# Six tiles in place of four for raw weights, in the room of a halved descriptor scratch

## The chip, the cores and the metric

The kernel runs on one core of a Trainium2 chip. The metric is the device time of one execution in microseconds (us). Before the change it is 770.23 us, the median of three runs (769.88 to 770.24).

The core has a tensor engine (PE, whose weight loads are shown apart as PEld), a vector engine (DVE), a scalar engine (ACT), a general engine (POOL, GpSimd) and a queue engine (SP, SyncE) that only issues transfers here. POOL issues transfers too: those that add to what they write.

## The reference

A decoder layer over 512 tokens of width 1024, in float32, batch 1. Two token mixers run side by side from one projection and are merged by sigmoid gates; a squared-ReLU MLP and a last norm follow.

```python
h = rms_norm(x, norm_mix)
proj = h @ w_in                       # 1024 -> 512 + 1024 + 6*128 + 48 + 2048
u, q, kc, vc, ksl, vsl, kwn, vwn, g_nsa, g_merge = split(proj)
y_pool = pool_mixer(u, w_pool, pool_scale)      # causal means over 2, 4, 8, 16 tokens
y_nsa = nsa_mixer(q, kc, vc, ksl, vsl, kwn, vwn, g_nsa, pe_k, pe_v, w_ck1, w_ck2, w_cv1, w_cv2)
g_a, g_b = split(sigmoid(g_merge))
x = x + (g_a * (y_pool @ w_proj_pool) + g_b * (y_nsa @ w_proj_nsa)) @ w_out
h = rms_norm(x, norm_mlp)
x = x + square(relu(h @ w_ff1)) @ w_ff2         # 1024 -> 4096 -> 1024
out = rms_norm(x, norm_final)
```

The second mixer has 16 heads of 64 in 2 groups. Each query attends to compressed keys (an MLP over blocks of 32 tokens), to selected blocks and to a window; at 512 tokens the selection and the window take in every causal key.

## The kernel before, in words

**Precision.** Every float32 product is split: each operand becomes a high part that PE multiplies quickly and a low part, the rest. ACT writes the high part (a copy that rounds) and DVE the low part (raw minus high). A product is three matmuls: high by high, high by low, low by high. So every weight tile that arrives from HBM as raw float32 costs one ACT and one DVE operation, or two of half the size, before PE can use it.

**Weight pipeline.** LD is the list of all loads in the order in which they are wanted, most of them 128 partitions by 1024 floats (512 KB). WL is the list of weight tiles in the order in which PE uses them. `emit_load` (L278) issues the next load on SP's queue (L297) into a tile tagged `raw`; there are RAW of these (L103), and they go round. `emit_prep_half` (L494) writes the high and low halves of the next weight tile (L524 on ACT, L527 on DVE); when a tile is done, its raw tile is free and one more load is issued. `gate_steps` (L411), `wo_steps` (L461) and `group_steps` (L372) do the same for the weights of the fast matrix products below (L428/L431, L471/L474, L390/L395). `ahead` (L542) is called between groups of matmuls and prepares the next weight if a pair of target tiles (wh/wl, wkt) is free for it. The load into a raw tile that has just been split waits on SP for the end of that split. Everything behind it on SP waits as well.

**The last stage.** From load MLP0 on, tiles are handed on by name: the first RAW of these loads take over the raw tiles (L287), a further tile `raw5` comes in when the attention's memory is free (L1599), and from then on a load is issued whenever a tile is given back (L323).

**Sums of weights.** The gates' projection, the output projection and the MLP use a seven-product scheme for products of two by two blocks, which needs sums of weight blocks (S1 to S4). Some of them are made in DRAM: SP copies one block into a DRAM tile (L335) and POOL adds the other with an accumulating transfer (L343); later the sum is loaded like any other weight. When each copy and each addition is issued hangs on the number of the load being issued (`sums_after`, L311, and the conditions at L301 to L306). POOL waits at an addition until the copy has landed.

**Order.** The program is written in one order. Between groups of matmuls it steps generators (`side`) that hold the evacuations, rope, the pooling mixer and so on. A planner then fixes the order of each engine: it takes instructions by their place in the program, moves some forward where `high_priority` says so, and starts one when by its own cost model its data and its tile are ready.

**Stages, by the profile's time.** A prologue (to about 16 us) normalises and transposes x; four loads are begun in it (L759 to L767), between the loads of x and of the constants. Until about 145 us the first projection runs: compressed keys (ck, wk0 to wk3), pooled channels (u0 to u3), keys, values (V0 to V2), first queries, the MLPs that compress keys and values (L997), wpool, and the gates' seven products (psV, L638). Until about 370 us the attention runs (L1378, L1400, L1410, L1423, L1440, L1474) with the rest of the projection as filler. Then the output projections, and from about 450 us the MLP in four parts, each with a first layer (L638) and a second (L1698).

**DMA scratch.** The program object (L2076) reserves part of each SBUF partition for the descriptors of transfers that POOL issues: 16,384 bytes where nothing is said.

## Time and profile before

| | |
|---|---|
| median of three runs | 770.23 us |
| span of the profiled execution | 767.4 us |
| PE busy | 756.7 us (99%) |
| DVE busy | 666.4 us (87%) |
| ACT busy | 511.1 us (67%) |
| POOL busy | 184.2 us (24%) |
| moved on SP's queue | 122.90 MB |
| moved by POOL's transfers | 26.22 MB |

The profile is of one execution of its own, from the first to the last instruction; for that execution it gives the span and no other time, so what lies around the span is seen only against the runs: 770.23 - 767.4 = 2.83 us. A line of the profile names the source line, the engine, the operation, what is written and read, shapes and count. "Idle before" is the time in which the engine stood still just before such an instruction, with what ended it. SPq and POOLq are the issuing of transfers. A busy PE is not PE at its peak, as matmuls overlap.

### The profile page before, as it was taken

The page shows a single profiled execution, that of the slowest core. Times are in us where ns is not written, and L with a number is a line of the kernel's source. Part 1 is how long each engine was busy: PE and PEld are TensorE (multiplying, and loading weights), DVE is VectorE, ACT ScalarE, POOL GpSimd, SP SyncE. Part 2 cuts the span into 40 slices and gives each one's busy share as a digit, 9 for nine tenths or more (in the row PEclk, how much of TensorE's full clock was granted, in tenths as well). Part 3 has the DMA queues.
Part 4 walks back from the last instruction along what each step waited for, and adds up shares of the span by engine and source line. Part 5 has one row for each costly group of instructions (what it writes and reads, how often), then busy time and mean ns, then how long its engine had stood idle before and what let it go on. Part 6 is the DMA issues. An engine that isn't in the chain of part 4 may idle for free.

```text
span 767.4 us, 13409 instructions
## 1 busy us (share of the span) xinstructions
PE 756.7 (99%) x4757; PEld 675.9 (88%) x4757; DVE 666.4 (87%) x1279; ACT 511.1 (67%) x977; POOL 184.2 (24%) x264
## 2 busy tenths in 40 slices
PE   9999999999999999999999999999999999999996
PEld 7889889888888888888889899989998999889985
DVE  7897999548988889989689689997989788978897
ACT  7766655328878888898745576954774477447754
POOL 4001010117746766574000200111111110111001
PEclk9999999999999999999999999999999999999999
DMA  9559993983051833371357965989998999799942
GB/s 308 165 143 266 251 230 108 257 214 115 15 176 52 158 56 70 56 138 60 116 186 220 324 111 185 287 219 299 310 259 222 314 303 257 215 325 294 293 171 110
DMA packets 119886, 150.76 MB, mean 196 GB/s; under 512 B 5782, under 2 KB 92346, under 8 KB 119611
## 3 DMA queue, kind: packets, MB, share of 16 engines
q1 hardware_dynamic: 98250, 122.90, 48.3%
q0 software_dynamic: 21280, 26.22, 22.8%
q8 instruction: 38, 0.62, 0.3%
q10 hardware_dynamic: 288, 0.79, 0.3%
q14 instruction: 30, 0.24, 0.1%
HBM read 145.16 MB, written 54.53 MB: 260 GB/s over the span
## 4 chain that ended last, share of the span: by engine, by line
PE 84%; DVE 9%; ACT 2%; DMA 2%; issue 1%; POOL 1%; SPq 0%; DVEq 0%; ACTq 0%; POOLq 0%
PE psB L638 20%; PE psB L1698 18%; PE psF L568 16%; PE psB L568 6%; PE psV L638 5%; PE psS L1378 4%; PE psT L1440 4%; PE psO L1474 4%; PE psB L1647 3%; DMA raw<-w_in 2%; PE psF L700 1%; DVE wl L527 1%; DVE PT L1456 1%; DVE P L1400 1%; DVE wkt L527 1%
## 5 line engine op out<-in xcount | busy, mean ns | idle before, releaser
L343 POOL DMA_DIRECT2D S<-w_ff x44 | 49.0, 1113 | 351.3 <-DMA S<-w_ff 290.3
L568 PE MATMUL psF<-R,wh 128*128 128x512 f32 x384 | 124.6, 400 | 0.0
L390 ACT ACTIVATE wh<-raw 128x1024 fp32r<-128x1024 f32 x73 | 77.1, 1058 | 70.0 <-PE psB L638 24.0
L1423 POOL TENSOR_SCALAR P<-P,sm,GT 128x128 f32<-128x128 f32 (+3 forms) x128 | 85.5, 724 | 68.8 <-DVE sm L1420 36.1
L395 DVE TENSOR_TENSOR wl<-raw,wh 128x1024 fp32r<-128x1024 f32 x73 | 88.9, 1219 | 12.7 <-ACT wh L390 12.2
L568 PEld LDWEIGHTS psF<-R,wh 128*128 128x128 f32 x384 | 68.8, 188 | 11.4 <-issue 0.2
L1410 ACT ACTIVATE P<-P,sm 128x128 f32<-128x128 f32 (+3 forms) x128 | 71.0, 557 | 9.9 <-DVE sm L1400 6.2
L568 PE MATMUL psF<-R,wl 128*128 128x512 f32 x192 | 75.5, 393 | 0.0
L524 ACT ACTIVATE wh<-raw 128x512 fp32r<-128x512 f32 (+1 forms) x76 | 45.1, 616 | 32.9 <-PE psF L568 21.2
L1400 DVE CUSTOM_DVE_ANT_0 P<-psS,cst 128x128 f32<-128x128 f32 (+3 forms) x128 | 59.3, 482 | 4.9 <-PE psT L1440 2.7
L390 ACT ACTIVATE w3h<-raw 128x1024 fp32r<-128x1024 f32 x37 | 39.2, 1059 | 34.0 <-PE psB L638 12.6
L527 DVE TENSOR_TENSOR wl<-raw,wh 128x512 fp32r<-128x512 f32 (+1 forms) x74 | 51.5, 707 | 9.2 <-ACT wh L524 8.9
L1451 ACT ACTIVATE PT<-psT 128x512 fp32r<-128x512 f32 (+2 forms) x96 | 49.0, 520 | 13.9 <-PE psT L1440 13.0
L1456 DVE TENSOR_TENSOR PT<-psT,PT 128x512 fp32r<-128x512 f32 (+2 forms) x96 | 56.2, 591 | 1.5 <-ACT PT L1451 1.3
L1440 PE MATMUL psT<-ident,P 128*128 128x128 f32 x320 | 50.1, 273 | 0.6 <-POOL rx L899 0.4
L395 DVE TENSOR_TENSOR w3l<-raw,w3h 128x1024 fp32r<-128x1024 f32 x37 | 45.1, 1220 | 4.7 <-ACT w3h L390 4.5
L1474 PE MATMUL psO<-PT,VV 128*128 128x256 f32 x320 | 48.5, 286 | 0.0
L1440 PEld LDWEIGHTS psT<-ident,P 128*128 128x128 f32 x320 | 39.6, 140 | 9.4 <-POOL rx L899 0.8
L638 PE MATMUL psB<-R,wh 128*128 128x256 f32 x336 | 46.3, 279 | 0.0
L1474 PEld LDWEIGHTS psO<-PT,VV 128*128 128x128 f32 x320 | 42.2, 188 | 1.3 <-ACT PT L1451 0.3
L638 PEld LDWEIGHTS psB<-R,wh 128*128 128x128 f32 x336 | 42.5, 188 | 0.2
L568 PEld LDWEIGHTS psF<-R,wl 128*128 128x128 f32 x192 | 36.0, 188 | 7.5
(442 smaller groups left out, 2083.7 us busy)
## 6 DMA issues: line engine op xcount, KB each, us to landing
raw<-w_ff SPq DMA_DIRECT2D x54, 512.0 KB, 6.2
S<-w_ff POOLq DMA_DIRECT2D x44, 512.0 KB, 8.2
raw<-S SPq DMA_DIRECT2D x44, 512.0 KB, 5.3
S<-w_ff SPq DMA_DIRECT2D x32, 512.0 KB, 7.3
raw<-w_in SPq DMA_DIRECT2D x31, 512.0 KB, 4.7
S<-S SPq DMA_DIRECT2D x12, 512.0 KB, 6.7
raw<-w_proj_nsa SPq DMA_DIRECT2D x8, 512.0 KB, 4.1
x<-x SPq DMA_DIRECT2D x7, 512.0 KB, 6.5
```

The costliest lines, as they stand in the source:

```text
L390: ACT.activation(h, t, AF.Copy)
L395: DVE.tensor_tensor(l, t, h.bitcast(F32), op=ALU.subtract)
L527: eng.tensor_tensor(l[:, sl], t[:, sl], h[:, sl].bitcast(F32), op=ALU.subtract)
L568: PE.matmul(ps, a, b, start=first and j == 0, stop=last and j == n - 1, skip_group_check=True)
L638: PE.matmul(out, w[u][:, k, 128 * f:128 * f + 128], moving[v][:, k, :], **kw)
L1400: DVE.tensor_tensor_reduce(out=P[:, o:o + n].rearrange("p (a c) -> p a c", c=128), in0=s, in1=m, scale=1.0, scalar=3e38, op0=ALU.add, op1= ...
L1410: last_exp[:] = [ACT.activation(c, c, AF.Exp, bias=sm[:, 0, e:e + 1], scale=-1.0, accum_out=sm[:, 1, e:e + 1])]
L1423: r = POOL.tensor_scalar(P[:, o:o + n], P[:, o:o + n], sm[:, 2, e:e + 1], GT[:, qb, c + e:c + e + 1], op0=ALU.mult, op1=ALU.mult)
L1440: PE.transpose(pt[:, 128 * j:128 * j + 128], P[:, 128 * j:128 * j + 128], ident)
L1456: return DVE.tensor_tensor(dL, src, dH.bitcast(F32), op=ALU.subtract)
L1474: PE.matmul(ps[:, qb % 2, :, :], VV[:, k, b, g, :], t[:, j, :, :], start=False, stop=last and j == len(kbs) - 1 and t is tL, skip_group_ch ...
L1698: PE.matmul(ps[f], self.Y.of(y)[u][:, 2 * g + k, 128 * f:128 * f + 128], w[v][:, k, :], start=first and g == k == u == v == 0, stop=g == k ...
```

## The change

RAW goes from four to six, so that six raw tiles go round, and seven with `raw5` in the last stage. Two more loads are issued at the end of the prologue, after the first halves of the first two projections and after the side work so far. The room, two tiles of 4,096 bytes in each partition, comes from the scratch for the descriptors of POOL's transfers, which is set to 8,192 bytes. All other places that use RAW follow it: the last stage takes over six tiles, and the tests `st["load"] > RAW + MLP0` and `st["kept"] == RAW` move with it. As additions and copies of the sums hang on load numbers, they are issued two loads earlier in the program too.

```diff
-    RAW = 4
+    RAW = 6
...
     next(first)
     next(first)
+    for _ in range(2):
+        emit_load()
     drain_side()
...
-    nc = bacc.Bacc("TRN2", target_bir_lowering=False, num_devices=1)
+    nc = bacc.Bacc("TRN2", target_bir_lowering=False, num_devices=1, dynamic_dma_scratch_size=8192)
```

## The prediction

> **What bounds the kernel now.** I read the page's busy times first, then busy time by stretch, then what TensorE (PE) waited for, then the instructions around its longest wait inside the work.

> ```profile
> span 767.4 us, 13409 instructions
> ...
> PE 756.7 (99%) x4757; PEld 675.9 (88%) x4757; DVE 666.4 (87%) x1279; ACT 511.1 (67%) x977; POOL 184.2 (24%) x264
> ...
> q0 software_dynamic: 21280, 26.22, 22.8%
> ...
> L524 ACT ACTIVATE wh<-raw 128x512 fp32r<-128x512 f32 (+1 forms) x76 | 45.1, 616 | 32.9 <-PE psF L568 21.2
> ...
> S<-w_ff POOLq DMA_DIRECT2D x44, 512.0 KB, 8.2
> ...
> rs<-rx SPq DMA_DIRECT2D x40, 64.0 KB, 2.0
> ```

> In the stretches the columns are the bounds and length of the stretch, then busy time and instructions of PE, PEld, DVE, ACT and POOL, the granted clock, the DMA share and GB/s.

> ```profile
> 0.00:16.00 16.00, 14.13 (x78) 10.46 (x79) 12.06 (x24) 11.60 (x22) 8.83 (x21) 1.00 0.95 311
> 16.00:32.00 16.00, 16.00 (x107) 14.44 (x106) 14.01 (x22) 13.42 (x24) 2.51 (x7) 1.00 0.66 183
> ...
> 32.00:64.00 32.00, 32.00 (x179) 28.44 (x178) 31.90 (x66) 20.18 (x37) 1.34 (x1) 1.00 0.65 186
> ...
> 80.00:96.00 16.00, 15.30 (x113) 14.34 (x112) 15.31 (x26) 10.23 (x16) 0.85 (x1) 1.00 0.93 245
> ...
> 176.00:368.00 192.00, 190.35 (x1231) 167.76 (x1230) 172.23 (x571) 164.38 (x446) 121.23 (x185) 1.00 0.38 87
> 368.00:752.00 384.00, 384.00 (x2441) 348.24 (x2441) 339.87 (x429) 236.27 (x336) 35.19 (x32) 1.00 0.86 244
> 752.00:767.40 15.40, 8.92 (x40) 7.03 (x38) 10.77 (x22) 6.86 (x20) 2.56 (x2) 0.88 0.36 137
> ```

> PE is the bound. It idles 767.4 - 756.7 = 10.7 us: 1.87 us before 16 us, 6.48 us after 752 us, and in between 0.70 us (80 to 96) and 1.65 us (the attention, 176 to 368). From 368 to 752, the output projection and the MLP, it is busy without a gap, although the DMA share there is 0.86. Deeper prefetch can only win idle time of PE that comes from late weights. So I ask what PE waited for between 16 and 752 us (total, times, longest):

> ```profile
> PE psS L1378 <- DVE sm L1400: 0.8, 2, 0.5
> PE psC L997 <- DVE wkt L527: 0.7, 1, 0.7
> PE psT L1440 <- POOL rx L899: 0.4, 1, 0.4
> PE psO L1465 <- DVE oT L1483: 0.2, 1, 0.2
> PE psT L1440 <- DVE PT L1456: 0.2, 1, 0.2
> ```

> No row names a transfer. Four are softmax, rope and evacuation work of the attention. One, 0.70 us at L997, is a weight tile whose low half (wkt) VectorE (DVE) delivered late. The instructions around it, taken from the views of four engines (start, length; in brackets the idle time before it and what ended it):

> ```profile
> 59.07 0.37 SPq L297 DMA_DIRECT2D raw<-w_in  x1
> ...
> 64.31 0.38 SPq L297 DMA_DIRECT2D raw<-w_cv  x1
> 68.33 0.37 SPq L297 DMA_DIRECT2D raw<-w_pool  x1
> ...
> 72.90 0.38 SPq L297 DMA_DIRECT2D raw<-w_in  x1
> ...
> 75.24 0.73 ACT L524 ACTIVATE wpl<-raw 128x256 fp32r<-128x256 f32 x2 [3.19 <-DMA raw<-w_pool]
> ...
> 78.29 1.06 ACT L428 ACTIVATE wh<-raw 128x1024 fp32r<-128x1024 f32 x1 [0.43 <-DMA raw<-w_in]
> ...
> 82.56 1.07 ACT L428 ACTIVATE wh<-raw 128x1024 fp32r<-128x1024 f32 x1 [1.68 <-PE psF L568]
> ...
> 75.69 0.76 DVE L527 TENSOR_TENSOR wpl<-raw,wpl 128x256 fp32r<-128x256 f32 x2 [2.02 <-ACT wpl L524]
> ...
> 85.60 1.23 DVE L431 TENSOR_TENSOR wl<-raw,wh 128x1024 fp32r<-128x1024 f32 x1
> 86.75 0.68 DVE L527 TENSOR_TENSOR wkt<-raw,wkt 128x512 fp32r<-128x512 f32 x1
> ...
> 87.95 0.68 DVE L527 TENSOR_TENSOR wkt<-raw,wkt 128x512 fp32r<-128x512 f32 x1
> ...
> 87.03 0.96 PE L997 MATMUL psC<-wkt,cA 128*128 128x256 f32 x6
> 88.69 0.50 PE L997 MATMUL psC<-wkt,cA 128*128 128x256 f32 x2 [0.70 <-DVE wkt L527]
> ```

> So there is one place where a late load reaches PE, by two steps: ScalarE (ACT) stood 3.19 us for wpool, DVE therefore stood 2.02 us, and from 75.69 on DVE works through a backlog until 88.63 with some 0.5 us of pause. PE loses 0.70 us at its end.

> **The change part by part.**

> *Six tiles and two more loads.* Nothing is computed more or less: the same loads of 512 KB, splits and matmuls. A finished split begins one load in the freed tile, so the waits of SP stay where they are and the load behind each becomes the one two places later in the list: load i is issued when load i-2 was. Wpool is number 19 and moves from 68.33 to the place of number 17, 59.07; number 20, the w_in load of 72.90, moves to that of number 18, 64.31. Wpool's load had landed when ACT began at 75.24, at most 6.9 us after its issue; at 59.07 it lands by 66.0, and ACT's 3.19 us and DVE's 2.02 us go. The w_in load's 0.43 us of ACT goes as well. Then the chain behind: ACT's conversion at 82.56 waits for PE and stays, so its DVE half (85.60) can start at 83.63 at the earliest, 1.97 us sooner, and the two wkt halves behind it follow by nearly as much, if DVE's order stays. PE wants the last at 87.99 and it would end at 88.63 - 1.97 = 86.7. The wait falls to nothing: **-0.70 us**. What is late next at that place is PE itself.

> Bounds of this term: 0, if DVE's backlog is refilled by other work, and -0.70, as no more is waited there. I take -0.70, because 1.97 is well over 0.70.

> *Sums.* The copies into DRAM and POOL's accumulating transfers for the sums S1 to S4 hang on load numbers, so they move two loads earlier as well, in the same order on SP and POOL. The tightest case is the gates' S2:

> ```profile
> 77.31 1.03 POOL L343 DMA_DIRECT2D S_g<-S_g  x1 [9.76 <-DMA S_g<-w_in]
> ...
> SPq L297 <- DMA S_g<-S_g: 2.3, 1, 2.3
> ```

> Its load held SP for 2.3 us until the sum had landed, and four rope copies stood behind it. Its copy begins some 9 us sooner now, while its load moves up by two places, about 6 to 8 us; that wait shrinks. PE did not feel it: 0 us. Cover gone, it would be 2.3 us on rope's copies, with PE still in the gates' matmuls.

> *Prologue.* Loads 4 and 5 need no freed tile any more, and two more follow them: about 1 MB more is in flight by 16 us. At the 311 GB/s of the first stretch that is 3.4 us of transfer. The next stretch shows DMA idle for 0.34 of 16 us, 5.4 us, so it fits in there. All of it is issued behind x, the first four weights and the constants on SP's queue, so the start of PE doesn't move: 0. Behind the loads on SP come rope's copies of the first k:

> ```profile
> 27.02 2.51 SPq L882 DMA_DIRECT2D rs<-rx  x4
> ...
> 34.81 0.41 DVE L899 TENSOR_TENSOR rs<-rs,cst 128x256 f32<-128x256 f32 x1
> ```

> They are issued by 29.53 and used at 34.81, which leaves 5.3 us less the landing (2.0 us is its median); even the full 3.4 us would nearly be absorbed. Bounds 0 to +0.1; I take 0.

> *Attention, output projection, MLP.* Here no wait of PE names a weight. Seven tiles in place of five (with the extra one of the last stage) let loads run further ahead, 0 us. Cover gone, a late tile of the MLP would cost PE what ACT waits, and PE shows none. For the shift of the attention's small waits in either direction, bounds -1.65 us (all its idle time) and, for a loss of like size, +1.65 us; I take 0, since their releasers are DVE and POOL results.

> *Smaller scratch.* It moves the constants by 8,192 bytes and the raw tiles grow by two of 4,096, so nothing shifts by an odd amount: 0. [...]

> Sum: 767.4 - 0.70 = 766.7 us of span. The median of the runs is 770.23, 2.83 us over the profiled span, which I take as what lies around it: 766.7 + 2.83 = **769.5 us**.

> **The rivals.**

> *A. No change, 770.2.* The loads begin earlier, but DVE's freed 2 us are filled by other work that the planner then finds ready, or another wait takes the place. For it: between 32 and 64 us DVE is busy 31.90 of 32 us and so has work queued. Against: at 73 us it idled with nothing to do.

> *B. All of PE's inner idle time shrinks, 767.9.* 770.23 - (0.70 + 1.65) = 767.88. For it: attention work is ordered by the same planner, and small waits move when anything before them does. Against: weights arrive long before their use there.

> *C. Slower: splits go ahead of what PE needs, 772.3.* The planner places instructions by when it believes their data is there. Weights that are there two loads sooner let splits of two more tiles, four halves of 0.68 us on DVE (the row of 86.75), come ahead of a result that PE waits for. DVE has only 0.1 us of room between 32 and 64 us, so that 4 x 0.68 = 2.7 us come back as a wait of PE: 770.23 + 2.7 - 0.70 = 772.3. It decides as soon as the halves moved ahead exceed PE's lead over DVE, which was below zero at 88 us. Against: a split also needs a free target, and ACT's 21.2 us of waiting for PE at L524 shows that targets come late, not data.

> [...]

> **How the numbers follow.** The forecast has 0.44, A 0.20, B 0.17, C 0.16, D 0.03. What this kernel's measurement can tell from no change is about 0.2%, 1.54 us. The forecast (-0.7) and A lie within it, B is faster, C and D slower; of the forecast's chance I leave 0.02 to each side. Same: 0.44 + 0.20 - 0.04 = 0.60; faster 0.17 + 0.02 = 0.19; slower 0.16 + 0.03 + 0.02 = 0.21. The likeliest case alone spans 768.8 to 770.2 (twice the gain, or none). The range runs from B less the 0.4 us by which the runs shown differ, 767.5, to C, 772.3; D and half of C's and a part of B's spread lie outside, under 0.2.

> **What would show it.** In the changed trace: wpool's load issued near 59 and the next w_in near 64 us; no wait of ACT for wpool; DVE without the 2.02 us of idle; no wait of PE at L997; PE full from 16 to 176 us and from 368 to 752 us as before; PE's busy time before 16 us still near 14.1; adds of POOL no slower than 1.2 us. I am wrong if PE shows a new wait behind a split of DVE before 176 us (C), if the sum of attention waits moves by over 1 us (B or its reverse), or if POOL's adds come spaced by their landing (D).

## The result, and the profile after

The changed kernel takes 778.35 us (median, 777.68 to 779.32) beside 770.24 us for the kernel before on the same chip: a ratio of 1.0105, 95% interval 1.0089 to 1.0121. It is **8.1 us slower**. The forecast was 769.5 us, and its range ended at 772.3. One of the ten executions of run e3 below took 1257.79 us at a mean granted clock of 0.557 and is left out of that run's ratio.

The profiled execution has a span of 776.9 us and a time of its own of 778.66 us. What lies around the span is therefore 1.76 us; the prediction had taken 2.83 from the runs' median, so the execution profiled before the change was about 1.1 us quicker than its median. Below, spans are compared with spans, and by them the change costs 9.5 us and not 8.1.

The page of the changed kernel, its busy times and POOL's additions:

```profile
span 776.9 us, 13408 instructions
...
PE 761.7 (98%) x4757; PEld 679.2 (87%) x4757; DVE 667.1 (86%) x1279; ACT 510.0 (66%) x977; POOL 183.9 (24%) x264
...
L343 POOL DMA_DIRECT2D S<-w_ff x44 | 49.0, 1115 | 370.9 <-DMA S<-w_ff 294.3
```

PE has the same 4757 instructions. Of the 9.5 us, 4.5 are idle time of PE (776.9 - 761.7 = 15.2 us in place of 10.7) and 5.0 are a longer busy time (761.7 in place of 756.7). The stretches of the changed kernel say where (bounds, length, busy time and instructions of PE, PEld, DVE, ACT and POOL, granted clock, DMA share, GB/s; a transfer's packets are counted in the stretch in which they begin, so a share can pass 1):

```profile
16.00:176.00 160.00, 159.96 (x977) 143.12 (x977) 132.32 (x241) 92.61 (x161) 16.85 (x26) 1.00 0.85 222
176.00:368.00 192.00, 189.79 (x1226) 166.79 (x1225) 172.54 (x568) 163.36 (x442) 120.74 (x185) 1.00 0.38 84
368.00:464.00 96.00, 91.67 (x496) 78.79 (x495) 69.96 (x106) 48.91 (x87) 6.75 (x6) 0.96 0.67 182
464.00:752.00 288.00, 288.00 (x1909) 264.72 (x1909) 260.63 (x312) 183.07 (x245) 28.53 (x26) 1.00 0.92 260
```

Between 16 and 176 us the predicted gain is there: PE idles 0.04 us, where it had idled 0.70. The attention idles 2.21 us (1.65 before). Between 368 and 464 us, the output projection, where PE had no gap at all, it now idles 4.33 us and the clock was 0.96. The MLP is full as before.

From here on I measure stages in each trace by their first and last matmuls, to about 0.1 us: first projection, from the first product (L700) to the first scores; attention, to the start of the last product with V; output projection, from the end of that product to the last transpose before the MLP.

```
                                     first projection  attention  output projection  span
before                                          164.3      192.4               88.7  767.4
after                                           163.0      193.6               97.4  776.9
```

What the first projection won, the attention gave back: the two together take 356.6 us, and 356.7 before. The loss is in the output projection.

**First projection.** The timeline of the changed kernel shows the load and the splits that wkt had stood behind:

```profile
58.69 0.37 SPq L297 DMA_DIRECT2D raw<-w_pool  x1
...
64.50 0.37 SPq L297 DMA_DIRECT2D raw<-w_in  x1
...
65.74 0.72 ACT L524 ACTIVATE wpl<-raw 128x256 fp32r<-128x256 f32 x2 [1.24 <-DMA raw<-w_pool]
...
66.20 0.76 DVE L527 TENSOR_TENSOR wpl<-raw,wpl 128x256 fp32r<-128x256 f32 x2 [0.41 <-ACT wpl L524]
```

Wpool's load left at 58.69 (68.33 before; predicted 59.07), DVE's 2.02 us of idle became 0.41, and no wait is left at this place. ACT's wait for wpool fell to 1.24 us and not to none, because the planner put the split sooner too. The split now stands ahead of the evacuation cg, for which PE waits; before it stood behind it. In this execution that cost PE 0.04 us at most. In the profiles of e5 and e9 below it cost more.

**Output projection.** What PE waited for there:

```profile
PE psB L1649 <- DVE wl L474: 2.6, 1, 2.6
PE psB L568 <- DVE wl L527: 1.3, 2, 0.7
```

All three waits are for low halves of weights, late on DVE. Followed back, DVE waited for ACT, and ACT for a load. The timeline of the changed kernel, all engines in order of time:

```profile
383.76 0.63 ACT L524 ACTIVATE W1H<-raw 128x512 fp32r<-128x512 f32 x1 [6.60 <-DMA raw<-w_out]
...
384.42 0.69 DVE L527 TENSOR_TENSOR W1L<-raw,W1H 128x512 fp32r<-128x512 f32 x1 [4.27 <-ACT W1H L524]
...
386.37 0.50 PE L568 MATMUL psB<-R,wl 128*128 128x512 f32 x1 [0.68 <-DVE wl L527]
...
392.74 1.06 ACT L471 ACTIVATE w3h<-raw 128x1024 fp32r<-128x1024 f32 x1 [5.23 <-DMA raw<-S_o]
...
407.95 1.16 ACT L524 ACTIVATE W1H<-raw 128x512 fp32r<-128x512 f32 x2 [3.57 <-DMA raw<-w_out]
...
415.08 0.58 PE L1649 MATMUL psB<-wl,R 128*128 128x256 f32 x1 [2.60 <-DVE wl L474]
```

The load that ACT waited for at 383.76 stands in the chain of waits (start, length):

```profile
374.73 9.01 DMA raw<-w_out
```

It took 9.01 us. In the kernel before, the same load was issued at 373.54 and ACT could split it at 377.39, 3.9 us later; the median of w_out's loads there, from issue to landing, is 4.1 us (timeline; then transfers: count, KB each, median):

```profile
377.39 1.15 ACT L524 ACTIVATE W1H<-raw 128x512 fp32r<-128x512 f32 x2 [1.42 <-DMA raw<-w_out]
```

```profile
raw<-w_out SPq DMA_DIRECT2D x7, 512.0 KB, 4.1
```

ACT stood at this split and did nothing else, so for 6.60 us it gave DVE nothing. (The longest wait, 2.60 us, also has a later load behind it: ACT stood 3.57 us at 407.95 for a split that the kernel before makes after 413. The last part of the experiments comes back to it.) What the first load had met is in the list of what SP issued at the attention's end, changed kernel first, then the kernel before:

```profile
361.10 0.52 SPq L297 DMA_DIRECT2D raw<-S  x1
361.75 0.50 SPq L335 DMA_DIRECT2D S<-S  x1
362.29 0.58 SPq L1735 DMA_DIRECT2D gB<-norm_mlp  x1
362.92 1.23 SPq L335 DMA_DIRECT2D S<-w_ff  x2
```

```profile
360.44 0.53 SPq L297 DMA_DIRECT2D raw<-S  x1
361.02 0.42 SPq L1733 DMA_DIRECT2D gB<-norm_mlp  x1
373.54 0.38 SPq L297 DMA_DIRECT2D raw<-w_out  x1
...
429.77 0.52 SPq L335 DMA_DIRECT2D S<-S  x1
430.33 1.25 SPq L335 DMA_DIRECT2D S<-w_ff  x2
```

Three copies of sums for the MLP's weights, which had gone out at 430 us, now go out at 362, with POOL's additions behind them. In stretches of 8 us, changed kernel first, then before:

```profile
368.00:376.00 8.00, 7.98 (x34) 5.98 (x33) 5.84 (x11) 7.94 (x15) 3.28 (x3) 1.00 1.06 230
376.00:384.00 8.00, 8.00 (x37) 6.63 (x36) 3.60 (x6) 0.87 (x2) 0.00 (x0) 1.00 1.09 258
```

```profile
368.00:376.00 8.00, 8.00 (x36) 6.50 (x36) 6.22 (x12) 6.87 (x13) 0.00 (x0) 1.00 0.13 47
376.00:384.00 8.00, 8.00 (x37) 6.60 (x36) 5.86 (x10) 3.85 (x7) 0.00 (x0) 1.00 0.59 185
```

The DMA engines go from a share of 0.13 and 0.59 to full, with three additions of POOL in the first stretch. ACT falls to 0.87 us of 8.

Why there: both lists begin with `raw<-S`. That is the load into `raw5`, the extra tile of the last stage. It waits for no split, so the planner issues it when the attention's memory comes free, some 60 us before its neighbours in the list of loads. The sums hang on load numbers, and what hangs on a load goes where the load goes. With four tiles raw5's load is number MLP0 + 4, which carries nothing. With six it is MLP0 + 6, the very number to which `sums_after` gives four copies and L305 up to three additions. Three of the copies went out with it, and three additions; the fourth copies a sum that has to be made first, and followed at 419.21 us.

**Clock.** PE's stretches of 2 us around its 2.60 us wait (busy time, granted clock, DMA share, GB/s):

```profile
412.00:414.00 2.00, 0.38 (x1) 1.00 0.75 164
414.00:416.00 2.00, 0.92 (x4) 0.59 1.16 197
416.00:418.00 2.00, 2.00 (x11) 0.50 1.12 270
418.00:420.00 2.00, 2.00 (x12) 0.50 0.12 37
420.00:422.00 2.00, 2.00 (x14) 0.71 0.86 262
```

After the wait PE ran at half clock until about 421 us, which by the clock column is 2 x (0.41 + 0.50 + 0.50 + 0.29) = 3.4 us, a little of it while PE still waited. So the output projection's 97.4 - 88.7 = 8.7 us are 4.3 us idle, about 3 us of clock by this reading, and 1 to 1.5 us that I don't assign. The clock's part is less sure than the idle time: of the changed kernel's four executions, the two with a mean granted clock of 0.993 took 778.66 and 779.32 us, and the one with 0.997 took 777.68, only 1.0 to 1.6 us less.

### The profile page after: what moved, and what is told of

It reads as the page before. It is cut to its first block, busy times and chain, and to the rows that moved or that the text cites. A ratio compares the mean times of both kernels' runs of the same rounds, so it can differ in the third digit from the quotient of the medians.

```text
span 776.9 us, 13408 instructions
## 1 busy us (share of the span) xinstructions
PE 761.7 (98%) x4757; PEld 679.2 (87%) x4757; DVE 667.1 (86%) x1279; ACT 510.0 (66%) x977; POOL 183.9 (24%) x264
## 3 DMA queue, kind: packets, MB, share of 16 engines
q0 software_dynamic: 21280, 26.22, 22.3%
## 4 chain that ended last, share of the span: by engine, by line
PE 82%; DVE 8%; ACT 4%; DMA 3%; issue 2%; POOL 1%; SPq 0%; ACTq 0%; POOLq 0%; DVEq 0%
PE psB L638 20%; PE psB L1700 17%; PE psF L568 17%; PE psV L638 5%; PE psB L568 4%; PE psT L1442 4%; PE psS L1380 3%; PE psO L1476 3%; PE psB L1649 3%; PE psV L568 2%; PE psF L700 2%; DMA raw<-w_out 1%; DVE P L1402 1%; DVE PT L1458 1%; PE psC L999 1%
## 5 line engine op out<-in xcount | busy, mean ns | idle before, releaser
L343 POOL DMA_DIRECT2D S<-w_ff x44 | 49.0, 1115 | 370.9 <-DMA S<-w_ff 294.3
L568 PE MATMUL psF<-R,wh 128*128 128x512 f32 x384 | 124.6, 400 | 0.0
L568 PEld LDWEIGHTS psF<-R,wh 128*128 128x128 f32 x384 | 68.9, 189 | 11.3
L568 PE MATMUL psF<-R,wl 128*128 128x512 f32 x192 | 75.6, 394 | 0.0
L524 ACT ACTIVATE wh<-raw 128x512 fp32r<-128x512 f32 (+1 forms) x76 | 45.0, 616 | 30.4 <-PE psF L568 21.2
L527 DVE TENSOR_TENSOR wl<-raw,wh 128x512 fp32r<-128x512 f32 (+1 forms) x74 | 51.7, 709 | 10.0 <-ACT wh L524 9.7
L395 DVE TENSOR_TENSOR w3l<-raw,w3h 128x1024 fp32r<-128x1024 f32 x37 | 45.1, 1220 | 5.5 <-ACT w3h L390 5.3
L568 PEld LDWEIGHTS psF<-R,wl 128*128 128x128 f32 x192 | 36.1, 188 | 7.5
## 6 DMA issues: line engine op xcount, KB each, us to landing
raw<-w_ff SPq DMA_DIRECT2D x54, 512.0 KB, 6.0
S<-w_ff POOLq DMA_DIRECT2D x44, 512.0 KB, 8.3
raw<-S SPq DMA_DIRECT2D x44, 512.0 KB, 6.1
S<-w_ff SPq DMA_DIRECT2D x32, 512.0 KB, 7.1
raw<-w_in SPq DMA_DIRECT2D x31, 512.0 KB, 5.9
S<-S SPq DMA_DIRECT2D x12, 512.0 KB, 6.6
raw<-w_proj_nsa SPq DMA_DIRECT2D x8, 512.0 KB, 4.2
x<-x SPq DMA_DIRECT2D x7, 512.0 KB, 7.1
```

The lines of the kernel that those rows point to most:

```text
L395: DVE.tensor_tensor(l, t, h.bitcast(F32), op=ALU.subtract)
L527: eng.tensor_tensor(l[:, sl], t[:, sl], h[:, sl].bitcast(F32), op=ALU.subtract)
L568: PE.matmul(ps, a, b, start=first and j == 0, stop=last and j == n - 1, skip_group_check=True)
```

## The experiments

Ratios stand against the kernel before, run beside them: its median was 770.26 us beside e1 to e4, 770.07 beside e5 to e8, 769.24 beside e9 to e11 and 769.05 beside e12.

**Is it the group of sums on raw5's load?** Four runs. The first gives the group of four copies and three additions to a load two later, the second brings the collision about with four tiles, the third sets the scratch alone, the fourth leaves out the prologue loads.

```diff
 # e1_burst_two_later: the changed kernel with
-        while i == MLP0 + 6 and len(begun) > 2:
+        while i == MLP0 + 8 and len(begun) > 2:
...
-            return {3: 1, 6: 4}.get(i - MLP0, 0)
+            return {3: 1, 8: 4}.get(i - MLP0, 0)
 # e2_four_tiles_burst_on_raw5: the kernel before (RAW = 4, full scratch) with
+        while i == MLP0 + 4 and len(begun) > 2:
...
+            return {3: 1, 4: 4}.get(i - MLP0, 0)
 # e3_scratch_alone: the kernel before with dynamic_dma_scratch_size=8192
 # e4_no_prologue_loads: the changed kernel without
-    for _ in range(2):
-        emit_load()
```

> The changed kernel, but the four copies for sums hang on load MLP0+8 in place of MLP0+6, so that they stand behind the second load after raw5's, as they do in the kernel before. Theory 1 (the burst hangs on raw5's load, which the planner moves up to 361 us, and takes the DMA engines from the loads of w_out): no PE wait at L1649, granted clock 1.00 throughout, DMA share of 368 to 384 us back from 1.07 to about 0.4; time 769 to 771, with the 0.7 us at L999 still won. Theory 2 (six raw tiles let ACT meet the splits of w_out too early, burst or not): a PE wait of 2 to 3 us at L1649 stays, 775 to 779. Theory 3 (the halved scratch holds up POOL, or the moved addresses cost): 775 to 779.

> The kernel before, four tiles and the full scratch, with one edit: the four copies hang on load MLP0+4, which there is the load into raw5. Theory 1: copies at about 361 us, DMA share of 368 to 384 us near 1, the same waits of ACT for w_out, PE waiting in 384 to 416 us; 774 to 780. Theory 2 and theory 3: 770, since neither the tiles nor the scratch are changed.

> The kernel before with the scratch of 8,192 bytes and nothing else. Theory 1 and theory 2: 769.9 to 770.6, POOL's additions at 1.1 us each as before. Theory 3: most of the 8 us is here, 775 to 779.

> The changed kernel without the two loads in the prologue: loads up to MLP0 run four ahead as before, the six tiles come in only at MLP0, and raw5's load is MLP0+6 again with the burst on it. Theory 1: the burst moves up to the end of the attention again; 774 to 780. Theory 2: loads of w_out are where they were before, so 770 to 771. The prologue loads alone as the cause (more transfers in flight early): 770 to 771.

```
                              median   ratio   95% interval     output projection
e1_burst_two_later            772.3    1.0026  1.0016 - 1.0036               91.0
e2_four_tiles_burst_on_raw5   778.84   1.0121  1.0095 - 1.0147               96.7
e3_scratch_alone              770.37   1.0000  0.9986 - 1.0013               88.7
e4_no_prologue_loads          775.9    1.0071  1.0050 - 1.0092               94.5
```

E1 takes back 6.0 of the 8.1 us, with six tiles, both prologue loads and the small scratch in place. In its trace PE idles 1.51 us between 368 and 464 us, in place of 4.33, at a clock of 1.00; so 2.8 of the 6.0 us are idle time, and the rest is busy time, the clock's part in it. E2 makes the same loss with four tiles and the full scratch. E3 shows that the scratch costs nothing. In e2, a stretch of all engines, what PE waited for, and a stretch of PE after it:

```profile
368.00:384.00 16.00, 16.00 (x72) 13.14 (x71) 8.24 (x14) 7.71 (x15) 3.28 (x3) 1.00 1.04 224
```

```profile
PE psB L568 <- ACT wh L524: 2.8, 1, 2.8
```

```profile
390.00:392.00 2.00, 2.00 (x7) 0.50 0.66 194
```

The DMA share is full as in the changed kernel, PE waits 2.8 us at one place, and the clock is halved again. In e1 the same stretch has a share of 0.41, against 0.36 before.

E4 expected loads four ahead again. That was not so: with six tiles a load no longer waits for the split just done, so loads run ahead without the prologue's two as well (a DMA share of 0.86 between 16 and 80 us, 0.76 before); the group meets raw5's load all the same. It lost 5.6 us and not 8.1. In its profiled execution (775.09 us) the clock did not fall, though the longest wait was the same 2.60 us (below); but its other executions, with mean clocks from 0.995 to 0.997, took 774.58 to 777.25 us, so the clock is not shown to make that difference.

**Is it that raw5's load goes forward, or the number of loads?** One edit to the changed kernel holds this load in its place in the list. The group stays on it.

```diff
 # e7_raw5_load_held
-            began[0] = nc.sync.dma_start(v[:, :, o:o + s.shape[2]], s)
+            with tc.issue_after(began[0].ins) if i == MLP0 + 6 else nullcontext():
+                began[0] = nc.sync.dma_start(v[:, :, o:o + s.shape[2]], s)
```

> The changed kernel, with one edit: the load into raw5 (number MLP0+6, which carries the group of four copies) is told to be issued after load MLP0+5, so that it can't be taken forward to the end of the attention. The group stays on the same load number. If the cause is that this one load hangs on no split and takes the group with it: the copies leave 361 to 363 us for about 425 us, the DMA share between 368 and 384 us falls from above 1.0 to under 0.5, no dip of the clock, total 771.5 to 773 us. If the cause is the number of loads in flight or the number of sums begun by then: no change, 778 us.

772.06 us, ratio 1.0025 (1.0015 to 1.0034): as e1, and as expected. The DMA share between 368 and 384 us is 0.37. So the first 6 us are settled from three sides: move the group, move the load, or make the collision without the tiles.

**What are the last 2 us?** In e1 PE still waits 1.2 us for a low half between 400 and 416 us. First theory: another copy (S_111_89, on load MLP0 - 2) meets the loads of x. Rival: loads and splits two further ahead.

```diff
 # e5_four_ahead_burst_two_later: e4 with the group on MLP0 + 8
 # e6_all_sums_two_later: e1 with
-            return i in EARLY or i in (26, 27, 33, 35, 36) or N1 + 3 <= i < N1 + len(FILL2) or i == MLP0 - 2
+            return i in EARLY or i in (26, 27, 33, 35, 36) or N1 + 3 <= i < N1 + len(FILL2)
...
-            return {3: 1, 8: 4}.get(i - MLP0, 0)
+            return {0: 1, 3: 1, 8: 4}.get(i - MLP0, 0)
 # e8_raw5_held_all_sums_later: e6 with the edit of e7
```

> Six tiles and the smaller scratch, without the two prologue loads, and the group of four copies and three additions hung on load MLP0+8. The first of three runs on what is left of the loss (2.0 us) once the group is moved. Theory R1 (the copy S_111_89, which hangs on load MLP0-2, meets the loads of x and w_out between 394 and 404 us): the copy stays where the ring of six puts it, so about as the kernel with both prologue loads, 771 to 773 us. Theory R2 (what costs is that loads, and with them the splits into W1H, run two further ahead than ScalarE's order has room for): fewer loads ahead at the end of the attention, so 769 to 770.5 us. The output projection took 91.0 us with the prologue loads and 88.7 before.

> The changed kernel with the group on load MLP0+8, and the copy S_111_89 moved from load MLP0-2 to MLP0 as well: all sums of the last stage hang two loads later than in the changed kernel, as many loads ahead of their use as with four tiles. R1: the copy leaves 398 us, SyncE issues it behind the last loads of x and w_out (after 405 us), ScalarE's waits for w_out's load (4.4 us with the copy at 398) fall under 2 us, TensorE's 1.2 us wait for a lower half goes, output projection 88.7 to 89.5 us, total 769.5 to 770.7 us. R2: no change against the run with the group alone moved, 772.3 +- 0.7 us.

> Both edits: raw5's load held behind load MLP0+5, and all sums of the last stage two loads later. R1 and the hoisted load as the whole cause: as the run with the sums alone moved or up to 0.5 us better, 769 to 770.5 us. If holding the load costs (it arrives at 361 us for nothing in the other kernels, and here about 425 us together with the others): 771 to 773 us.

E6 took 772.23 us (1.0027; 1.0017 to 1.0038) and e8 772.14 (1.0023; 1.0014 to 1.0032): no gain. The first theory, R1, falls. E5 took 770.36 us (1.0005; 0.9990 to 1.0019), as the rival, R2, had said: without the prologue loads most of the 2 us go. R2 doesn't say which step costs PE time; e6's trace does. The timelines of e6, then of the kernel before:

```profile
402.63 1.15 ACT L524 ACTIVATE W1H<-raw 128x512 fp32r<-128x512 f32 x2 [1.07 <-DMA raw<-w_out]
...
408.38 1.15 ACT L524 ACTIVATE W1H<-raw 128x512 fp32r<-128x512 f32 x2 [1.38 <-DMA raw<-w_out]
...
409.75 0.39 PE L1649 MATMUL psB<-wl,R 128*128 128x256 f32 x1 [0.68 <-DVE wl L474]
```

```profile
413.71 1.14 ACT L524 ACTIVATE W1H<-raw 128x512 fp32r<-128x512 f32 x2
...
423.13 1.16 ACT L524 ACTIVATE W1H<-raw 128x512 fp32r<-128x512 f32 x2 [3.55 <-DMA raw<-w_out]
```

The splits of wo12 and wo13 have a fixed target (W1H, W1L) and wait for nothing but their load. When the load is there sooner, the planner puts them sooner: 11 and 15 us earlier, between the splits that PE needs next, each with ACT's wait for the load in front. This is the split of 407.95 in the changed kernel too. In e8 PE waits 2.22 us for a low half here, with no group near it, so the 2.60 us belong in part to this cause (theory R3). The two splits held in their place, with and without the prologue loads:

```diff
 # e9_w1_splits_held: e1, and e10_four_ahead_splits_held: e5, each with
-            ACT.activation(h, t, AF.Copy)
+            last_hi[0] = ACT.activation(h, t, AF.Copy)
...
-                conv[0] = ACT.activation(h[:, sl], t[:, sl], AF.Copy)
+                with behind(last_hi[0]) if WL[i][0] in ("wo12", "wo13") else nullcontext():
+                    conv[0] = ACT.activation(h[:, sl], t[:, sl], AF.Copy)
```

> The changed kernel with the group on load MLP0+8, and the splits of two residual weights (wo12 and wo13, into W1H and W1L) told to come behind the split that precedes them in the program, so that the planner can't take them forward between the splits of the output projection's first half. Theory R3 for the last 2 us (formed after the sums of the last stage had been moved without effect): with six tiles these loads land two loads earlier, ScalarE then splits them at 402.6 and 408.4 us in place of 413.7 and 423.1, waits for their loads in order, and the split wl that TensorE needs at 409 comes 0.7 to 2.2 us late. If R3 holds: no wait of TensorE for wl between 400 and 432 us, TensorE full in both windows of 16 us, total 770 to 771 us. If what is left comes from the two loads more in flight themselves: no change, 772.3 us.

> The kernel without the prologue loads, group on load MLP0+8 (770.36 us), with the same two splits held. R3: its profile too had TensorE waiting 0.8 us for wl, so 769.2 to 770.2 us. If the prologue loads are what the last 2 us come from, and not the splits: no change, 770.4 us.

```
                               median   ratio   95% interval     first proj.  attention  output proj.
e9_w1_splits_held              769.92   1.0010  1.0002 - 1.0019        165.9      193.7          89.2
e10_four_ahead_splits_held     769.05   0.9998  0.9989 - 1.0008        163.0      192.6          89.2
```

PE is full in e9's output projection:

```profile
400.00:416.00 16.00, 16.00 (x102) 14.51 (x101) 14.76 (x21) 9.21 (x12) 1.17 (x1) 1.00 0.95 281
416.00:432.00 16.00, 16.00 (x122) 15.24 (x121) 16.00 (x20) 7.65 (x11) 0.00 (x0) 1.00 0.55 186
```

R3 holds: the wait is gone, the output projection is back to 89.2 us, and e9's ratio is 1.6 thousandths under e1's, some 1.2 us (the two intervals just touch). E9's profile fell on its slowest run (772.6 us; the other ten lie between 769.6 and 770.4), and its long first projection is that run's: PE waited 1.31 us for cg, shown below. E5's profile, its second slowest of twelve (772.99 us), has a wait of 1.57 us at the same place. In both, wpool's split stands on ACT ahead of cg, as in the changed kernel, and ACT waited 2.0 to 2.5 us for wpool's load in place of 1.24. So this order costs some executions time and others none. What the prologue loads still cost, e9 against e10, is 0.9 us with intervals that overlap. The attention takes 193.5 to 193.7 us in the six profiles with six tiles and prologue loads, and 192.6 to 193.1 in the three without. I have not found the cause of that difference.

No version beats the kernel before: e10 has no gap of PE left between 16 and 176 us but 0.12 us, and is the same by its interval.

**Five tiles.** If the coincidence of two numbers is the cause, RAW = 5 avoids it, with raw5's load at MLP0 + 5 and the group left on MLP0 + 6.

```diff
 # e11_five_tiles: the changed kernel with
-    RAW = 6
+    RAW = 5
...
-    for _ in range(2):
+    for _ in range(1):
         emit_load()
 # e12_five_tiles_wpool_split_held: e11 with the evacuation cg kept, and
+                with behind(cg_made[0]) if WL[i][0] == "wpool" else nullcontext():
+                    conv[0] = ACT.activation(h[:, sl], t[:, sl], AF.Copy)
```

> Five tiles in place of six, one prologue load in place of two, the smaller scratch; the group of four copies is left on load MLP0+6. The load into raw5 is then number MLP0+5 and carries no sums, so if the coincidence of the two numbers is the cause, the copies go out after 420 us, the DMA share between 368 and 384 us stays under 0.5 and the time is 770 to 772 us (one W1 split is still early). If the loss grows with the number of tiles and of loads ahead, about half of it: 774 us.

775.47 us, ratio 1.0092 (1.0076 to 1.0107): a miss in the total. In the output projection the expectation holds: 90.9 us, and a DMA share of 0.37 between 368 and 384 us. The loss is in the first projection, 168.4 us. The timeline of e11:

```profile
70.21 0.72 ACT L524 ACTIVATE wpl<-raw 128x256 fp32r<-128x256 f32 x2 [3.56 <-DMA raw<-w_pool]
...
72.42 0.85 PE L1037 MATMUL psM<-cg,w2d 128*128 128x64 f32 x6 [3.58 <-ACT cg L1027]
```

Here the planner put the split of wpool ahead of cg, an evacuation that PE was waiting for, and the load was late (issued at 64.63 us). In the kernel before, cg came first, and ACT's 3.19 us for the same load cost PE nothing there and 0.70 us at 88 us. The clock was 0.89 in the 16 us around it, by that column another 16 x 0.11 = 1.8 us.

> The five-tile kernel with one edit: ScalarE's split of wpool is told to come behind its evacuation cg, for which TensorE waited 3.58 us at 72 us there. In the five-tile kernel wpool's load left at 64.63 us and the planner had put its split ahead of cg, so cg stood behind a wait of 3.56 us for a DMA; the granted clock was 0.89 in the 16 us around it. If that order is what five tiles lost by in the first projection (3.6 us of wait and 1.8 us of clock): no wait for cg, clock 1.00 between 64 and 80 us, first projection 163 to 164 us in place of 168.4, total 770 to 771.5 us. If the loss follows the number of tiles or the group of sums after all: 774 us or more.

772.75 us, ratio 1.0054 (1.0040 to 1.0068): better by 2.7 us, half of what was expected. The wait for cg went, but the split still stood in ACT's order before another evacuation (GT, L1122): ACT waited 2.28 us for the load, PE 2.2 us for GT, the clock was 0.89 again, and the first projection took 166.3 us where 163 to 164 were expected. So the order on ACT accounts for 2.7 us; that holding the split behind GT as well would win the rest was not run.

## Why the prediction was wrong

**Six tiles and two more loads: right.** Every load left two places sooner, wpool at 58.69 us, and PE's 0.70 us went. By stages the first projection is 1.3 us shorter than before in the changed kernel, by PE's idle time 0.66 us. The total shows nothing of it.

**"PE did not feel it: 0 us" (sums) and "let loads run further ahead, 0 us" (output projection): the steps that failed.** The first worked through the tightest sum of the gates and took it that all others move "two loads earlier as well, in the same order". That holds in the program and not in time. One load in the list, raw5's, is issued 60 us ahead of its neighbours, and the row for it stands in the trace of before: `raw<-S` alone at 360.44 us. A shift by two numbers hung seven transfers on it, and six went out with it. The term was 0 and measured 6.0 us (after against e1; e2 makes it 8.6 with four tiles).

The second step looked for waits of PE that name a weight, found none and concluded that earlier weights change nothing. But PE's freedom from gaps rested on ACT's order, and an earlier load changed that order. The term was 0 and measured 1.2 us (e1 against e9). "Cover gone, a late tile … would cost PE what ACT waits" was a bound that I had for the MLP and did not carry into the sum.

**Attention, 0 within 1.65: within its bounds.** It measured +1.2 us with the prologue loads. The cause is open.

**Prologue, 0 to +0.1: too narrow, though not settled.** The bounds asked only what the transfers cost beside x and rope's copies. The two loads also set how early the later splits come: 1.6 us between e1 and e5, 2.5 us between after and e4, and 0.9 us between e9 and e10, where the splits are held and the intervals overlap.

**Scratch and rival D: 0 was right.** E3, with the scratch alone halved, is 1.0000, and POOL's additions take 1115 ns each in the changed kernel, 1113 before. No run shows POOL's transfers held up by the smaller scratch, the case that has 0.03 in the forecast as D: in the changed kernel POOL issues two additions in the 2.13 us from 371.96 us on, while the median from issue to landing is 8.3 us.

**Rival C named the second mechanism and not the place.** "Splits go ahead of what PE needs" is what e6 shows and e9 undoes. That C's time of 772.3 us is also e1's is chance: it was worked out from four halves on DVE before 176 us. There the order did change, on ACT, by wpool's own split: it cost the changed kernel's profiled execution 0.04 us at most, those of e9 and e5 1.3 and 1.6 us, and that of e11 3.6 us. No rival held the group of copies. The sign that the prediction named, "PE full … from 368 to 752 us as before", is the one that pointed at the cause.

## What to carry to other kernels

When a change shifts the number on which other work hangs, list for every number what it carries and when its load is really issued, and look for loads that wait for nothing. A buffer that comes sooner also changes the order that a planner makes: an engine that stands at a load holds back all that stands behind it in its order (ACT for 6.60 us here), so a split whose load is uncertain belongs behind the evacuations that the tensor engine needs. Where the engine that bounds the kernel has no gap, as here from 368 us on, more prefetch has nothing to win and can lose (8.7 us in the output projection here), so ask what it does to the engines that feed it.

## What the runs showed of the hardware

The granted clock fell to half in or after short waits, and not with each of them. In e4 a wait at the line of the changed kernel's longest one, equally long (2.60 us), left it at 1.00; in e9 one of half the length (1.31 us) halved it. In e5 a wait of 1.57 us at e9's place, with the same eight matmuls behind it, left it at 1.00; the mean clock of that execution is 0.998, as in the kernel before, and e9's is 0.996. The wait and PE's stretches of 2 us, first in e4, then in e9, and last the wait in e5:

```profile
PE psB L1647 <- DVE wl L474: 2.6, 1, 2.6
```

```profile
412.00:414.00 2.00, 0.33 (x2) 1.00 1.18 191
414.00:416.00 2.00, 2.00 (x19) 1.00 0.85 273
```

```profile
69.86 1.08 PE L1038 MATMUL psM<-cg,w2d 128*128 128x64 f32 x8 [1.31 <-ACT cg L1028]
```

```profile
70.00:72.00 2.00, 2.00 (x14) 0.75 0.45 142
72.00:74.00 2.00, 2.00 (x8) 0.50 1.03 290
```

```profile
PE psM L1035 <- ACT cg L1025: 1.6, 1, 1.6
```

So a wait of 1.3 to 3.6 us had a second price of 1.7 or 3.4 us of lost clock, or none; what that costs in time is less sure, as said above.

Copies within DRAM with additions behind them, 1.5 MB of copies and 1.5 MB of additions, all issued between 361.75 and 374.1 us by SP and POOL, made the load of 374.73 us land after 9.01 us, beside a median of 4.1. The DMA share was 1.06 and 1.09 in the two stretches of 8 us from 368 to 384 us. With the group moved (e1), that share was 0.41 over the 16 us, and ACT could split the same load 3.5 us after its issue (374.39 to 377.91 us).
